# The first norms of a hybrid encoder block in a new order, with GpSimd's weight subtractions in eight pieces

## The chip, the cores and the metric

The kernel runs on one core of a Trainium2 chip. A core has a matrix engine (TensorE, in the profile PE for the products and PEld for its weight loads), VectorE (DVE), ScalarE (ACT), GpSimd (POOL) and SyncE (SP), whose queue issues most of the DMAs. Each engine works through its own list of instructions in a fixed order, and they wait for each other by semaphores. The metric is the device time of one execution in microseconds (us). The kernel before took 1527.0 us, the median of three runs (1525.58 to 1529.02).

## The reference

One block of depth 1 on 1040 tokens (16 learned meta tokens and 1024 frames) of width 1024, in float32. What matters here is the start of it:

```python
def rmsnorm(x, g):
    xf = x.astype(jnp.float32)
    y = xf * lax.rsqrt(jnp.mean(xf * xf, axis=-1, keepdims=True) + EPS)
    return (y * g.astype(jnp.float32)).astype(x.dtype)

def token_mixer(u, w_in, ...):
    proj = up @ w_in          # up: the normed stream, padded in front
    (ml_q, ml_k, ml_v, ml_o, ml_i, ml_f, rt_q, rt_k, rt_v, rt_g) = jnp.split(proj, offs, axis=-1)
    ...                       # mLSTM heads with gates, retention heads with rotary q and k
    return (mixed @ w_out)[:, n_pad:]

h = h + token_mixer(rmsnorm(h, norm_mix_g[l]), w_in[l], ...)
h = h + channel_mixer(rmsnorm(h, norm_ffn_g[l]), ...)
return rmsnorm(h, norm_final_g)[:, N_META:]
```

The stream is normed, projected to queries, keys, values, output gates and input/forget gates, run through four mLSTM heads and four retention heads, projected back, and followed by a gated MLP.

## The kernel before, in words

The stream lies transposed in SBUF: model width on the partitions (eight blocks of 128, in two tiles `x11` and `x12` for the first half of the tokens and `x21` and `x22` for the second), tokens along the free axis. To keep float32 accuracy in single-pass matmuls each operand is split in two parts, `hi` (a cast by ScalarE) and `lo` (the original minus `hi`, by VectorE or GpSimd), and a product is the sum of three: hi by hi, hi by lo, lo by hi.

The first norm goes through the tokens in five ranges r = 0 to 4 (`RNG`: 144, 128 and 256 tokens of the first half, 272 and 256 of the second). For each range:

- `norm_sums(r)`: the squares (`sqr`, by ScalarE, and for r < 2 by VectorE too), sums of squares by VectorE, a product with a column of ones on TensorE (`pca`, one column per 128 tokens), the root on ScalarE and the reciprocal on VectorE (`rcola`).
- `norm_split(r)`: the reciprocals are spread over the partitions by TensorE (`pra`, the rows), VectorE scales the stream (`scalar_tensor_tensor`, eight passes), ScalarE casts the high halves (`u11h`, `u12h`, ...), VectorE subtracts the low halves (`u11l`, ...).

What TensorE can do meanwhile are products of ranges that are ready: `v4_group(c)` makes the values and gate inputs of chunk c (`pv`, 48 matmuls of 264 columns; 8 chunks of 128 tokens, and the meta tokens as chunk 0), with weights `w0hi` and `w0lo` that `v0_split` makes; `q4_group(i, ...)` makes one head's queries (i = 0) or keys (i = 1) for a range of tokens (`pq`, 24 matmuls), with weights that `need(("q4", i))` loads and splits (`parts`: `hi_q` by ScalarE, `lo_q` by VectorE).

After the five ranges come sums and differences of the token blocks (`S1` to `S4`, for a Winograd-like scheme of the big products), their splits, the output gate of head 4 (`po4x`, `po4y`), the rotation of its queries and keys with two tables `A1` and `A2` (`tables_load`, 520 KB each, in buffers that the sums `s1` used before), and the gates: rows of input and forget gates through scans on VectorE (`gates`, `gsm`), a trip through a DRAM buffer `scr`, and then the chunkwise scan of the heads.

The order of instructions on each engine isn't that of the program text: the code is recorded and a scheduler of the framework (a timeline that it computes when the kernel is built) decides, by its own estimate of readiness, which recorded instruction of an engine comes next. `after(later, first)` adds an order between two instructions to what the data demand, and no wait of its own on the same engine. From the output gate of head 4 on (`dealt[0] = True`) the kernel's own planner deals out the work. `last[...]` keeps the latest instruction of a kind, for use in `after`.

The names in the lists of instructions carry a number for the range or the chunk: `pra4` are the rows of range 4, `pv4_5` the values of chunk 5, `pq40116` the queries of range (1, 16).

Of the kernel before, what the change touches and what calls it, by code (L numbers as in the profile page):

```python
# [10 lines left out]
F32 = mybir.dt.float32  # L11
# [6 lines left out]
P = 128  # L18
# [71 lines left out]
def body(ctx, tc, h_in, vecs, cst, mask_in, rot, w_v0, w_vp, w_g, w_out, w_up, w_gate, w_down, out):  # L90
# [381 lines left out]
    def parts(key, pairs, src):  # L472
        for i, (hi, lo) in enumerate(pairs):
            m = AC.copy(hi, src[:, i * HB:(i + 1) * HB])
            if not dealt[0]:
                after(m, last["first"])
        yield
        for i, (hi, lo) in enumerate(pairs):
            V.tensor_tensor(lo, src[:, i * HB:(i + 1) * HB], hi.bitcast(F32), ALU.subtract)
        done.add(key)  # L480

    def pairs_of(nm, n):
# [334 lines left out]
    def rms_sums(ss, t0, t1, nm, col, tag, more=()):  # L817
        n = t1 - t0
        o = n % P
        subs = ([(0, P, o)] if o else []) + [(i, P, P) for i in range(o, n, P)]  # L820
        pc = rps("pc" + nm, tag)
        for i, (o, w, _) in enumerate(subs):
            for a in (ss, *more):
                PE.matmul(pc[:w, i:i + 1], a[:, o:o + w], cs[:, C_M01 + P - 1:C_M01 + P], start=a is ss, stop=a is (ss, *more)[-1])
        ns = len(subs)
        last["sqrt"] = AC.activation(col[:, :ns], pc[:, :ns], AF.Sqrt, bias=epsc, scale=1.0 / D)
        last["recip"] = V.reciprocal(col[:, :ns], col[:, :ns])
        return n, subs, pc, col, nm

    def rms_rows(got, rb, tag):  # L830
        n, subs, pc, col, nm = got
        pr = rps("pr" + nm, tag)
        x = max(0, n - 512)
        for i, (o, _, w) in enumerate(subs):
            dst = pr[:, o - x:o - x + w] if o >= x else pc[:, 8:8 + w]
            PE.matmul(dst, col[:, i:i + 1].to_broadcast([P, P]), ident[:, :w], start=True, stop=True)
# [8 lines left out]

    norms = {}

    def norm_sums(r):
        half, j0, j1 = RNG[r]
        n = j1 - j0  # L850
        xs = [xf[f"{half + 1}{i + 1}"][:, :, j0:j1] for i in (0, 1)]
        sq = [x[:, :, j0:j1] for x in sqs]
        m = AC.activation(sq[0], xs[0], AF.Square)
        if r:
            after(m, last["sqrt"])
        if r < 2:
            m = V.tensor_tensor(sq[1], xs[1], xs[1], ALU.mult)
# [12 lines left out]
        norms[r] = xs, rms_sums(ss[0], 0, n, f"a{r}", tmp.tile([P, 5], F32, tag="rcol", name=f"rcola{r}"), "tr", ss[1:])  # L870

    def norm_split(r):
        half, j0, j1 = RNG[r]
        xs, got = norms.pop(r)
        pr = rms_rows(got, None, "upd")
        parts_ = [[u[:, :, j0:j1] for u in UB[f"{half + 1}{i + 1}"]] for i in range(2)]
        for i, x in enumerate(xs):
            for k in range(4):
                last["scale"] = V.scalar_tensor_tensor(x[:, k], x[:, k], vec[:, V_MIX + 4 * i + k:V_MIX + 4 * i + k + 1], pr, ALU.mult, ALU.mult)
            m = AC.copy(parts_[i][0], x)  # L880
# [24 lines left out]
    def v0_split():  # L905
        for i in range(2):
            after(AC.copy(w0hi[i], w0raw[i]), last["sqrt"])
            G.tensor_tensor(w0lo[i], w0raw[i], w0hi[i].bitcast(F32), ALU.subtract)

    def quads(dst, pv, n):  # L910
        yield
# [7 lines left out]
    def v4_group(c, tag, between=None):  # L919
        t0, L = CH[c]  # L920
        nv = 264
        pv = pp(f"pv4_{c}", tag)
        if c == 0:
            for i in range(2):
                for j in range(4):
                    PE.matmul(pv[32 * j:32 * j + 32, :nv], ug[:, 4 * i + j, :], w0raw[i][:, j * nv:(j + 1) * nv],
                                     start=i == 0, stop=i == 1, tile_position=(0, 32 * j))
            t = vz[:META, 264:264 + nv]
            spawn(quads(t, pv, nv))
            V.tensor_copy(gts[:META, :, 0, :], t[:, DV:].rearrange("p (a b) -> p a b", a=2))  # L930
            return
        half = c > 4
        j0 = t0 - 512 * half
        for i, j in ((0, 0), (0, 1), (1, 0)):
            if i and between:
                between()
            for kb in range(KB):
                u = UB[f"{half + 1}{kb // 4 + 1}"][i]
                o = kb % 4 * nv
                PE.matmul(pv[:, :nv], u[:, kb % 4, j0:j0 + L], (w0hi, w0lo)[j][kb // 4][:, o:o + nv], start=i + j + kb == 0, stop=i == 1 and kb == KB - 1, skip_group_check=True)  # L940
        AC.copy(vtile[4][half][:, (c - 1) % 4 * VW:(c - 1) % 4 * VW + DV], pv[:, :DV])
        V.tensor_copy(gts[:, :, c, :], pv[:, DV:nv].rearrange("p (a b) -> p a b", a=2))
# [818 lines left out]
    norm_sums(3)  # L1761
    for c in (3, 4):
        v4_group(c, next(ring0))
# [767 lines left out]
```

## Time and profile before

| | |
|---|---|
| median of 3 runs | 1527.0 us |
| the profiled execution: its own time, its span | 1527.2 us, 1525.4 us |
| TensorE busy | 1489.9 us, 98% of the span |
| VectorE busy | 1090.1 us, 71% |
| ScalarE busy | 755.6 us, 50% |
| GpSimd busy | 73.6 us, 5% |
| moved between HBM and SBUF | 161 GB/s over the span |

The profile is one execution. Times are counted from the start of the span. A row of the timeline gives start, length, engine, line, operation, written tile <- read tiles, shape, and how many like instructions were merged; in square brackets stands how long the engine had been idle and which instruction released it. A row of waits gives who waited for whom, the total, how often and the longest. A row of windows gives a stretch of time and the busy time of each engine in it, then the clock granted to TensorE, the DMA share and GB/s.

### The profile page before, as it was taken

The page shows a single profiled execution, that of the slowest core. Times are in us where ns is not written, and L with a number is a line of the kernel's source. Part 1 is how long each engine was busy: PE and PEld are TensorE (multiplying, and loading weights), DVE is VectorE, ACT ScalarE, POOL GpSimd, SP SyncE. Part 2 cuts the span into 40 slices and gives each one's busy share as a digit, 9 for nine tenths or more (in the row PEclk, how much of TensorE's full clock was granted, in tenths as well). Part 3 has the DMA queues.
Part 4 walks back from the last instruction along what each step waited for, and adds up shares of the span by engine and source line. Part 5 has one row for each costly group of instructions (what it writes and reads, how often), then busy time and mean ns, then how long its engine had stood idle before and what let it go on. Part 6 is the DMA issues. An engine that isn't in the chain of part 4 may idle for free.

```text
span 1525.4 us, 25488 instructions
## 1 busy us (share of the span) xinstructions
PE 1489.9 (98%) x9929; PEld 1350.0 (88%) x9929; DVE 1090.1 (71%) x2087; ACT 755.6 (50%) x1453; POOL 73.6 (5%) x153
## 2 busy tenths in 40 slices
PE   6999999999999999999999999999999999999997
PEld 6998999999999999986888988999999999888887
DVE  7785868678777677856867787767666666778657
ACT  4465655554655455553454565444444444444443
POOL 1000000000000000000000001222220000000000
PEclk9999999999999999999999999999999999999999
DMA  6022255323532355696333247888772224933313
GB/s 232 8 88 51 86 159 194 111 82 114 186 119 98 125 166 189 195 398 255 111 112 134 80 124 241 197 208 200 189 183 77 83 79 160 369 105 110 97 42 111
DMA packets 104586, 223.81 MB, mean 147 GB/s; under 512 B 10520, under 2 KB 33760, under 8 KB 104288
## 3 DMA queue, kind: packets, MB, share of 16 engines
q1 hardware_dynamic: 89824, 191.68, 37.7%
q0 software_dynamic: 8448, 23.07, 7.6%
q10 hardware_dynamic: 6192, 7.41, 1.4%
q8 instruction: 78, 1.28, 0.4%
q14 instruction: 44, 0.36, 0.1%
HBM read 178.05 MB, written 67.15 MB: 161 GB/s over the span
## 4 chain that ended last, share of the span: by engine, by line
PE 89%; DVE 6%; DMA 2%; ACT 2%; issue 1%; SPq 0%; DVEq 0%; ACTq 0%
PE pdx L902 3%; PE pdx L901 3%; PE pdx L900 3%; PE pup_x L901 2%; PE pup_x L902 2%; PE pga_x L900 2%; PE pup_x L900 2%; PE pga_x L901 2%; PE pga_x L902 2%; PE pdy L902 2%; PE pdy L901 2%; PE pdy L900 2%; PE n L1570 2%; PE pwx L902 2%; PE u L1568 2%; PE pv L940 2%
## 5 line engine op out<-in xcount | busy, mean ns | idle before, releaser
L780 ACT CAST hi_up<-raw_up 128x512 fp32r<-128x512 f32 (+1 forms) x52 | 36.4, 719 | 107.4 <-PE pga_z L901 61.1
L781 DVE TENSOR_TENSOR lo_ga<-fraw_ga,hi_ga 128x512 fp32r<-128x512 f32 (+1 forms) x52 | 41.9, 809 | 37.3 <-ACT hi_ga L780 37.1
L781 DVE TENSOR_TENSOR lo_up<-raw_up,hi_up 128x512 fp32r<-128x512 f32 (+1 forms) x52 | 41.3, 810 | 38.0 <-ACT hi_up L780 37.2
L900 PE MATMUL pup_x<-uh_g,hi_up 128*128 128x256 f32 (+1 forms) x240 | 67.2, 282 | 1.2 <-ACT uh_g L1928 1.2
L901 PE MATMUL pup_x<-ul_g,hi_up 128*128 128x256 f32 (+1 forms) x240 | 67.4, 282 | 0.1
L902 PE MATMUL pup_x<-uh_g,lo_up 128*128 128x256 f32 (+1 forms) x240 | 66.4, 282 | 0.0
L781 DVE TENSOR_TENSOR lo_d<-rd,hi_d 128x1024 fp32r<-128x1024 f32 (+1 forms) x34 | 37.7, 1114 | 32.8 <-ACT hi_d L780 32.7
L780 ACT CAST hi_ga<-fraw_ga 128x512 fp32r<-128x512 f32 (+1 forms) x52 | 36.4, 719 | 45.3 <-PE pup_z L901 21.9
L902 PE MATMUL pdx<-uh_d,lo_d 128*128 128x512 f32 (+1 forms) x156 | 57.9, 375 | 0.0
L901 PE MATMUL pdx<-ul_d,hi_d 128*128 128x512 f32 (+1 forms) x156 | 57.8, 374 | 0.0
L780 ACT CAST hi_d<-rd 128x1024 fp32r<-128x1024 f32 (+1 forms) x34 | 32.3, 959 | 49.3 <-PE pdy L901 32.5
L902 PE MATMUL pdy<-uh_d,lo_d 128*128 128x512 f32 x132 | 51.9, 393 | 0.0
L901 PE MATMUL pdy<-ul_d,hi_d 128*128 128x512 f32 x132 | 51.7, 392 | 0.0
L900 PE MATMUL pdx<-uh_d,hi_d 128*128 128x512 f32 (+1 forms) x156 | 48.5, 372 | 0.0
L900 PE MATMUL pdy<-uh_d,hi_d 128*128 128x512 f32 x132 | 47.9, 389 | 0.0
L900 PE MATMUL pga_x<-uh_g,hi_ga 128*128 128x512 f32 x120 | 47.5, 396 | 0.0
L901 PE MATMUL pga_x<-ul_g,hi_ga 128*128 128x512 f32 x120 | 47.5, 396 | 0.0
L900 PEld LDWEIGHTS pup_x<-uh_g,hi_up 128*128 128x128 f32 x240 | 45.3, 189 | 2.3 <-ACT uh_g L1928 1.4
L902 PE MATMUL pga_x<-uh_g,lo_ga 128*128 128x512 f32 x120 | 47.1, 393 | 0.0
L901 PEld LDWEIGHTS pup_x<-ul_g,hi_up 128*128 128x128 f32 x240 | 45.4, 189 | 1.0 <-DVE ul_g L1929 0.3
L902 PEld LDWEIGHTS pup_x<-uh_g,lo_up 128*128 128x128 f32 x240 | 44.8, 189 | 0.8
L1637 DVE SCALAR_TENSOR_TENSOR mx<-tr,vec,sig 128x386 f32<-128x386 f32 (+2 forms) x42 | 24.0, 572 | 20.7 <-PE tr L1629 16.0
(1684 smaller groups left out, 5752.4 us busy)
## 6 DMA issues: line engine op xcount, KB each, us to landing
raw_up<-w_up_d SPq DMA_DIRECT2D x22, 512.0 KB, 4.4
fraw_ga<-w_gate_d SPq DMA_DIRECT2D x22, 512.0 KB, 4.1
acts<-cv SPq DMA_DIRECT2D x44, 256.0 KB, 4.2
wsd<-w_down_d POOLq DMA_DIRECT2D x44, 256.0 KB, 6.6
rd<-wsd SPq DMA_DIRECT2D x22, 512.0 KB, 3.6
raw_w<-w_out_d SPq DMA_DIRECT2D x20, 512.0 KB, 6.8
wsw<-raw_w SPq DMA_DIRECT2D x32, 256.0 KB, 3.7
raw_m<-w_out_d SPq DMA_DIRECT2D x14, 512.0 KB, 4.0
```

Of the source, the lines that this page charges most:

```text
L780: AC.copy(hi[:, o:o + n], x)
L781: V.tensor_tensor(lo[:, o:o + n], x, hi[:, o:o + n].bitcast(F32), ALU.subtract)
L900: m.append(PE.matmul(pt, ah, xh_, start=first and k == 0, stop=False, skip_group_check=True))
L901: PE.matmul(pt, ah, xl_, start=False, stop=False, skip_group_check=True)
L902: m.append(PE.matmul(pt, al, xh_, start=False, stop=last and k == n - 1, skip_group_check=True))
L940: PE.matmul(pv[:, :nv], u[:, kb % 4, j0:j0 + L], (w0hi, w0lo)[j][kb // 4][:, o:o + nv], start=i + j + kb == 0, stop=i == 1 and kb == KB - ...
L1568: PE.matmul(up[:, :nv], kw[:L], v, start=True, stop=True)
L1570: PE.matmul(pn[:L, :nv], pt[:L, :L], v, start=True, stop=c == 0)
L1637: return V.scalar_tensor_tensor(dst, tr[:, x0 - t0:x1 - t0], vec[:, g:g + 1], sig(b, p)[:, x0 - a0:x1 - a0], ALU.mult, ALU.mult)
```

## The change

Six things are done in the first hundred microseconds, all in the code that records the first norms and products:

1. `v0_split`: GpSimd's two subtractions of 128 x 1056 become eight of 128 x 264.
2. The second range's sums and its rows (`norm_rows(1)`) are both placed inside the products of chunk 1, ahead of those with the low halves; those products are ordered behind the rows.
3. The query and key weights are asked for later (`need` moves behind the products of chunk 2), and their low halves (`lo_q`) are ordered behind the latest sum of squares.
4. The query and key products of the first 272 tokens are made together by `q4_pair`: pass by pass (hi by hi, hi by lo, lo by hi) for both, and not product by product for one and then the other.
5. The third range's sums stand between the second and the third pass, its rows between the queries and the keys of the third pass.
6. The later squares of ranges 2 and 3 are ordered behind the low halves before them (`last["pace"]`) instead of behind the reciprocal; the copy of the first keys stands behind the third range's cast.

The core of the diff:

```diff
@@ parts
-            V.tensor_tensor(lo, src[:, i * HB:(i + 1) * HB], hi.bitcast(F32), ALU.subtract)
+            m = V.tensor_tensor(lo, src[:, i * HB:(i + 1) * HB], hi.bitcast(F32), ALU.subtract)
+            if not dealt[0]:
+                after(m, last["added"])
@@ norm_sums
-                after(m, last["recip"])
-            V.tensor_tensor(sq[0][:, 0:2], sq[0][:, 0:2], sq[0][:, 2:4], ALU.add)
+                after(m, last["pace"] if r in (2, 3) else last["recip"])
+            last["added"] = V.tensor_tensor(sq[0][:, 0:2], sq[0][:, 0:2], sq[0][:, 2:4], ALU.add)
...
+    def norm_rows(r):
+        norms[r] += (rms_rows(norms[r][1], None, "upd"),)
@@ v0_split
-            G.tensor_tensor(w0lo[i], w0raw[i], w0hi[i].bitcast(F32), ALU.subtract)
+            for o in range(0, 1056, 264):
+                G.tensor_tensor(w0lo[i][:, o:o + 264], w0raw[i][:, o:o + 264], w0hi[i][:, o:o + 264].bitcast(F32), ALU.subtract)
@@ v4_group
+                if i and between:
+                    after(m, last["rows"])
@@ new
+    def q4_pair(half, j0, j1, tags, between):
+        w = [need(("q4", i), 1 - i) for i in range(2)]
+        pt = [pp(f"pq4{i}{half}{j0}", tags[i])[:, :j1 - j0] for i in range(2)]
+        for p, (a, b) in enumerate(((0, 0), (0, 1), (1, 0))):
+            if p == 2:
+                between()
+            for i in range(2):
+                if p == 2 and i:
+                    norm_rows(2)
+                for kb in range(KB):
+                    u = UB[f"{half + 1}{kb // 4 + 1}"][b]
+                    m = PE.matmul(pt[i], w[i][kb // 4][a][:, kb % 4 * P:(kb % 4 + 1) * P], u[:, kb % 4, j0:j1], start=p + kb == 0, stop=p == 2 and kb == KB - 1, skip_group_check=True)
+                    if p == 2:
+                        after(m, last["rows" if i else "sums"])
+        AC.copy(raws[0][:, half * 512 + j0:half * 512 + j1], pt[0])
+        yield
+        after(AC.copy(raws[1][:, half * 512 + j0:half * 512 + j1], pt[1]), last["cast"])
@@ the first products
-    v4_group(1, next(ring0), lambda: norm_sums(1))
-    need(("q4", 0), 1)
+    def second():
+        norm_sums(1)
+        norm_rows(1)
+    v4_group(1, next(ring0), second)
     norm_split(1)
     v4_group(0, next(ring0))
     v4_group(2, next(ring0))
-    norm_sums(2)
-    q4_group(0, 0, 0, 272, next(ring0))
+    third = norm_sums(2, True)
+    need(("q4", 0), 1)
+    pair = q4_pair(0, 0, 272, [next(ring0), next(ring0)], third)
+    next(pair)
     norm_split(2)
-    q4_group(1, 0, 0, 272, next(ring0))
+    next(pair, None)
```

What becomes of it on the engines is decided by the scheduler. Behind the first hundred microseconds the lists of the two kernels are the same but for two products in the middle of TensorE's. At three places they differ in what the prediction speaks of.

VectorE's list from the second range's squares on, before: `sqr1` the squares, `u11l` and `u12l` the low halves of the first range, `lo_q4` the weights' low halves, `rcola1` and `rcola2` the reciprocals of ranges 1 and 2.

```order
L857 TENSOR_TENSOR sqr1_133<-x12_121 128x4x128
L887 COPY ug_117<-x11_122 128x128
L884 TENSOR_TENSOR u11l_125<-x11_122,u11h_124 128x4x144
L887 COPY ug_117<-x12_121 128x128
L884 TENSOR_TENSOR u12l_127<-x12_121,u12h_126 128x4x144
L479 TENSOR_TENSOR lo_q4_0_0_290<-raw_q4_0_201,hi_q4_0_0_289 128x512 x2
L479 TENSOR_TENSOR lo_q4_1_0_298<-raw_q4_1_203,hi_q4_1_0_297 128x512 x2
L827 RECIPROCAL rcola1_267<-rcola1_267 128x1
L865 TENSOR_TENSOR sqr0_132<-sqr0_132,sqr1_133 128x4x256
L868 TENSOR_TENSOR sqr0_132<-sqr0_132 128x2x256
```

The same place of VectorE's list now:

```order
L895 TENSOR_TENSOR u12l_127<-x12_121,u12h_126 128x4x144
L829 RECIPROCAL rcola1_273<-rcola1_273 128x1
L890 SCALAR_TENSOR_TENSOR x11_122<-x11_122,vec_72,pra1_285 128x128 x4
L890 SCALAR_TENSOR_TENSOR x12_121<-x12_121,vec_72,pra1_285 128x128 x4
L956 COPY gts_116<-pv4_1_254 128x2x4
L927 TENSOR_TENSOR vz_111<-pv4_0_309,vz_111 16x264
L895 TENSOR_TENSOR u11l_125<-x11_122,u11h_124 128x4x128
L927 TENSOR_TENSOR vz_111<-pv4_0_309,vz_111 16x264
L895 TENSOR_TENSOR u12l_127<-x12_121,u12h_126 128x4x128
L867 TENSOR_TENSOR sqr0_132<-sqr0_132,sqr1_133 128x4x256
L927 TENSOR_TENSOR vz_111<-pv4_0_309,vz_111 16x264
L870 TENSOR_TENSOR sqr0_132<-sqr0_132 128x2x256
```

The reciprocals and the scaling of range 1 moved ahead of the weights' low halves, which now follow behind these rows.

TensorE's list at the rows of the last range (`pra4`), before:

```order
L891 MATMUL pq410272_562<-u12l_127,hi_q4_1_0_297 128x256
L892 MATMUL pq410272_562<-u12h_126,lo_q4_1_0_298 128x256
L836 MATMUL pra4_588<-cs_73,rcola4_528 128x128 x2
L940 MATMUL pv4_5_631<-w0hiq_106,u21h_130 128x264 x4
L940 MATMUL pv4_5_631<-w0hik_107,u22h_128 128x264 x4
L940 MATMUL pv4_5_631<-w0lo0_108,u21h_130 128x264 x4
L940 MATMUL pv4_5_631<-w0lo1_109,u22h_128 128x264 x4
```

and now, where the values of chunks 5 and 6 and the first queries of the second half come first (46 and 12 matmuls in all):

```order
L901 MATMUL pq40116_691<-u21h_130,hi_q4_0_0_354 128x256
L902 MATMUL pq40116_691<-u21l_131,hi_q4_0_0_354 128x256
L952 MATMUL pv4_5_637<-w0hik_107,u22l_129 128x264 x4
L952 MATMUL pv4_6_664<-w0hik_107,u22l_129 128x264 x2
L838 MATMUL pra4_594<-cs_73,rcola4_534 128x128 x2
L952 MATMUL pv4_6_664<-w0hik_107,u22l_129 128x264 x2
```

The last range's rows moved behind nearly all products of chunks 5 and 6.

SP's list of DMAs behind the loads of the stream, before (`A1_4` and `A2_4` are the rotation tables, `raw_q0a`, `raw_vp0` and `raw_q0b` weights):

```order
L328 DMA raw_o4b_303<-w_g_d 128x512 x2
L1102 DMA A1_4_851<-rot_d 128x1040
L1103 DMA A2_4_852<-rot_d 128x1040
L328 DMA raw_q0a_873<-w_g_d 128x1024
L328 DMA raw_vp0_21_1262<-w_vp_d 128x1024
L328 DMA raw_vp0_22_1264<-w_vp_d 128x1024
```

and now:

```order
L328 DMA raw_o4b_368<-w_g_d 128x512 x2
L328 DMA raw_q0a_879<-w_g_d 128x1024
L328 DMA raw_vp0_21_1268<-w_vp_d 128x1024
L328 DMA raw_vp0_22_1270<-w_vp_d 128x1024
L1134 DMA A1_4_857<-rot_d 128x1040
L1135 DMA A2_4_858<-rot_d 128x1040
```

The tables moved behind three weight loads, two of which wait for products of TensorE.

More of the change, by code (lines that the diff above doesn't have):

```diff
@@ L823, in rms_sums @@
             for a in (ss, *more):
-                PE.matmul(pc[:w, i:i + 1], a[:, o:o + w], cs[:, C_M01 + P - 1:C_M01 + P], start=a is ss, stop=a is (ss, *more)[-1])
+                last["sums"] = PE.matmul(pc[:w, i:i + 1], a[:, o:o + w], cs[:, C_M01 + P - 1:C_M01 + P], start=a is ss, stop=a is (ss, *more)[-1])
         ns = len(subs)
@@ L835, in rms_rows @@
             dst = pr[:, o - x:o - x + w] if o >= x else pc[:, 8:8 + w]
-            PE.matmul(dst, col[:, i:i + 1].to_broadcast([P, P]), ident[:, :w], start=True, stop=True)
+            last["rows"] = PE.matmul(dst, col[:, i:i + 1].to_broadcast([P, P]), ident[:, :w], start=True, stop=True)
         if x:
@@ L846, in body, with norm_sums @@
     norms = {}
-    def norm_sums(r):
+    def norm_sums(r, late=False):
         half, j0, j1 = RNG[r]
@@ L866, in norm_sums, with sums @@
             if r:
-                after(m, last["recip"])
-            V.tensor_tensor(sq[0][:, 0:2], sq[0][:, 0:2], sq[0][:, 2:4], ALU.add)
+                after(m, last["pace"] if r in (2, 3) else last["recip"])
+            last["added"] = V.tensor_tensor(sq[0][:, 0:2], sq[0][:, 0:2], sq[0][:, 2:4], ALU.add)
             ss = [sq[0][:, k] for k in range(2)]
-        norms[r] = xs, rms_sums(ss[0], 0, n, f"a{r}", tmp.tile([P, 5], F32, tag="rcol", name=f"rcola{r}"), "tr", ss[1:])
+        def sums():
+            norms[r] = xs, rms_sums(ss[0], 0, n, f"a{r}", tmp.tile([P, 5], F32, tag="rcol", name=f"rcola{r}"), "tr", ss[1:])
+        if late:
+            return sums
+        sums()
+    def norm_rows(r):
+        norms[r] += (rms_rows(norms[r][1], None, "upd"),)
     def norm_split(r):
         half, j0, j1 = RNG[r]
-        xs, got = norms.pop(r)
-        pr = rms_rows(got, None, "upd")
+        if len(norms[r]) < 3:
+            norm_rows(r)
+        xs, got, pr = norms.pop(r)
         parts_ = [[u[:, :, j0:j1] for u in UB[f"{half + 1}{i + 1}"]] for i in range(2)]
@@ L879, in norm_split @@
                 last["scale"] = V.scalar_tensor_tensor(x[:, k], x[:, k], vec[:, V_MIX + 4 * i + k:V_MIX + 4 * i + k + 1], pr, ALU.mult, ALU.mult)
-            m = AC.copy(parts_[i][0], x)
+            m = last["cast"] = AC.copy(parts_[i][0], x)
             if r == 0:
@@ L939, in v4_group @@
                 o = kb % 4 * nv
-                PE.matmul(pv[:, :nv], u[:, kb % 4, j0:j0 + L], (w0hi, w0lo)[j][kb // 4][:, o:o + nv], start=i + j + kb == 0, stop=i == 1 and kb == KB - 1, skip_group_check=True)
+                m = PE.matmul(pv[:, :nv], u[:, kb % 4, j0:j0 + L], (w0hi, w0lo)[j][kb // 4][:, o:o + nv], start=i + j + kb == 0, stop=i == 1 and kb == KB - 1, skip_group_check=True)
+                if i and between:
+                    after(m, last["rows"])
         AC.copy(vtile[4][half][:, (c - 1) % 4 * VW:(c - 1) % 4 * VW + DV], pv[:, :DV])
```

## The prediction

> **What bounds the kernel now.** I read the page first, then the table by windows, then the timeline of the first 125 us, since the list of instructions changes only there.
>
> ```profile
> span 1525.4 us, 25488 instructions
> PE 1489.9 (98%) x9929; PEld 1350.0 (88%) x9929; DVE 1090.1 (71%) x2087; ACT 755.6 (50%) x1453; POOL 73.6 (5%) x153
> PE   6999999999999999999999999999999999999997
> ```
>
> TensorE is busy in 98% of the span, and one of its weakest slices is the first. A change in the first 100 us counts only by how much later or earlier it lets TensorE go on for the rest. The windows of that stage (PE, PEld, DVE, ACT, POOL busy; then granted clock, DMA share, GB/s):
>
> ```profile
> 28.00:31.50 3.50, 3.50 (x17) 3.50 (x18) 3.47 (x9) 2.44 (x4) 0.09 (x1) 0.51 0.03 7
> 35.00:40.00 5.00, 5.00 (x44) 5.00 (x43) 4.20 (x6) 1.15 (x3) 0.00 (x0) 1.00 0.00 0
> 53.40:84.50 31.10, 30.52 (x261) 29.58 (x261) 29.39 (x39) 17.22 (x27) 3.30 (x2) 1.00 0.16 52
> ```
>
> From 28 to 31.5 TensorE works at half its clock. From 53.4 to 84.5 it is full, but VectorE too: 29.39 of 31.10 us. That second queue is what the change runs into.
>
> **The front, 0 to 53 us.** The waits that the new order is about:
>
> ```profile
> 12.49 2.44 POOL L908 TENSOR_TENSOR w0lo<-w0raw,w0hik 128x1056 fp32r<-128x1056 f32 x1
> 12.79 2.68 DVE L857 TENSOR_TENSOR sqr<-x 128x512 f32<-128x512 f32 x1
> 15.54 1.87 PE L824 MATMUL pca<-cs,sqr 128*128 128x1 f32 x8 [0.99 <-DVE sqr L857]
> 17.01 2.49 DVE L479 TENSOR_TENSOR lo_q<-raw_q,hi_q 128x512 fp32r<-128x512 f32 x4
> 26.24 0.71 PE L836 MATMUL pra<-cs,rcola 128*128 128x128 f32 x4 [1.22 <-DVE rcola L827]
> 27.88 1.08 PE L940 MATMUL pv<-w0hiq,u11h 128*128 128x264 f32 x4 [0.93 <-ACT u11h L880]
> ```
>
> VectorE's square of the second range took 2.68 us, where a product of that shape takes 2.49 / 4 = 0.62: it ended 15.47, 0.5 us after GpSimd's subtraction (14.93). In pieces of 2.44 / 4 = 0.61 us it need wait for one piece only: 12.79 + 0.61 + 0.62 = 14.0. That removes TensorE's wait of 0.99. Bounds: 0.99, or nothing if VectorE stays out until all eight pieces are through. I take 0.99.
> The Trainium skill's page "SBUF — State Buffer" (section "Who interferes with whom") says that a VectorE instruction with two SBUF inputs and a GpSimd instruction that reads SBUF exclude each other for a whole instruction, whichever issued first. This trace agrees with the 2.68; no row yet shows which of the two goes next between two pieces.
>
> The third range's squares, sums and rows now come behind the first query and key products, so the waits 1.22 and 0.93 go, and with them, if nothing else stops TensorE, the half clock: 3.5 x 0.49 = 1.7 us. New waits come, from these rows:
>
> ```profile
> 23.50 2.15 DVE L879 SCALAR_TENSOR_TENSOR x<-x,vec,pra 128x128 f32<-128x128 f32 x8 [0.41 <-PE pra L836]
> 27.22 0.61 ACT L880 CAST u11h<-x 128x512 fp32r<-128x512 f32 x1
> 28.68 1.66 DVE L879 SCALAR_TENSOR_TENSOR x<-x,vec,pra 128x256 f32<-128x256 f32 x4
> 30.37 1.05 ACT L880 CAST u11h<-x 128x1024 fp32r<-128x1024 f32 x1 [0.98 <-DVE x L879]
> 52.78 0.61 PE L836 MATMUL pra<-cs,rcola 128*128 128x128 f32 x4
> 53.42 3.22 DVE L879 SCALAR_TENSOR_TENSOR x<-x,vec,pra 128x256 f32<-128x256 f32 x8 [0.99 <-PE pra L836]
> 53.71 0.65 PE L940 MATMUL pv<-w0hik,u22h 128*128 128x264 f32 x4
> 58.57 0.65 PE L940 MATMUL pv<-w0hik,u22l 128*128 128x264 f32 x4
> ```
>
> From a row multiply to its first scaling pass 53.42 - 52.78 = 0.64 us. A matmul takes (58.57 - 53.71) / 40 = 0.12. After the second range's rows TensorE has 8 products and a ninth small one (1.3 us) before it needs the new high half: 0.64 + 2.15 / 2 + 0.61 = 2.3, so 1.0 of waiting. After the third's it has the two row multiplies and 8 query-low products (0.5 + 1.0): 0.64 + 1.66 + 1.05 = 3.35, so 1.9. Each can be 0.5 longer, where ScalarE still has casts and copies queued ahead. The front: -0.99 - 1.22 - 0.93 - 1.7 + 1.0 + 1.9 = -1.9 us (from -3.0, were the new waits half as long, to about 0, were the clock to fall again). GpSimd's eight starts for two, and 24 + 24 products in another order, cost TensorE nothing else: the number of matmuls is the same.
>
> **The last norm, 53 to 88 us.** Before, the rows of the last range (52.78) stand ahead of the value products of chunks 5 and 6. Now 58 matmuls stand ahead of them: 46 value and 12 query and key products, 58 x 0.12 = 7.0 us. They come at 52.78 + 7.0 - 1.9 = 57.9, and VectorE scales from 58.5 on instead of 53.4: 5.1 later. It has idled before that, but what follows is the same list of work: two differences, low halves, sums, four more low halves, up to the rotation. VectorE's waits in that stretch:
>
> ```profile
> DVE gates L1213 <- ACT gates L1212: 2.2, 1, 2.2
> DVE x L879 <- PE pra L836: 1.0, 1, 1.0
> DVE uS1l L1787 <- ACT uS1h L1786: 0.8, 1, 0.8
> DVE uS3l L1787 <- ACT uS3h L1786: 0.5, 1, 0.5
> DVE gts L942 <- ACT v4hi L941: 0.3, 1, 0.3
> ...
> ```
>
> A later VectorE no longer waits for the last three: -1.6. No other idle time can take up the lag; 3.5 of 5.1 us remain. (Bounds: 5.1 if nothing is swallowed; nothing at all if the scaling starts 3.5 earlier than I find.)
>
> **The rotation tables.** SP's queue has them behind three weight loads now:
>
> ```profile
> 73.96 0.33 SPq L1102 DMA_DIRECT2D A<-rot_d  x1
> 75.12 0.33 SPq L1103 DMA_DIRECT2D A<-rot_d  x1
> 83.55 0.80 SPq L328 DMA_DIRECT2D raw_vp<-w_vp_d  x2
> 84.46 0.70 DVE L1180 TENSOR_TENSOR qT<-rawq,A 128x528 f32<-128x528 f32 x1
> ...
> A<-rot_d SPq DMA_DIRECT2D x2, 520.0 KB, 4.7
> raw_vp<-w_vp_d SPq DMA_DIRECT2D x2, 512.0 KB, 4.5
> raw_q0a<-w_g_d SPq DMA_DIRECT2D x1, 512.0 KB, 3.6
> ```
>
> Before, they landed some 5 us ahead of their use (75.12 + 4.7 against 84.46). Now they follow raw_vp, which waits for TensorE's meta products: 83.55 - 1.9 and, as TensorE meets VectorE's lag, perhaps a microsecond more. Issued at some 83.5 and landed 4.7 to 5.7 later, behind 1.5 MB of the other loads, they come at 88.2 to 89.2; VectorE is ready at 84.46 + 3.5 = 88.0. I take 1.0 us of waiting (0 if they land first, 1.7 if both come last).
>
> **To the end.** Why TensorE follows VectorE here:
>
> ```profile
> 88.45 1.28 ACT L1212 ACT_TABLE_LOAD   x1
> 89.75 0.36 ACT L1212 ACTIVATE gates<-pg,gsm 36x128 f32<-36x128 f32 x1
> 106.91 0.38 SPq L1267 DMA_DIRECT2D scr<-gates  x1
> 124.08 0.80 PE L1523 MATMUL s<-qT,kT 128*128 128x128 f32 x2 [2.62 <-DVE pt L1547]
> PE pe L1240 <- DVE gsm L1236: 0.8, 1, 0.8
> PE pe L1239 <- DVE gates L1232: 0.6, 1, 0.6
> PE s L1523 <- DVE pt L1547: 2.6, 1, 2.6
> ```
>
> Rotation, gate rows, scans, the trip of the gates through memory (106.91) and the first scan step are one chain on VectorE. TensorE waits for it three times (0.6, 0.8, 2.6), so a gain of TensorE ahead of it only lengthens these waits, and a lag of the chain arrives whole. ScalarE's table load and tanh (1.28 + 0.36) make the gate wait 1.8 instead of 2.2: -0.4. Sum: 5.1 - 1.6 + 1.0 - 0.4 = +4.1 us. The profiled execution took 1527.2 us (1.8 around the span); 1527.2 + 4.1 = 1531.3, and as it lies 0.2 over the median of 1527.0, I predict 1531.1.
>
> **Rivals.** (1) The other side: the front decides. If the last scaling starts by 55.0 (53.42 + 1.6), VectorE swallows the lag, and the front's gain stays: 1527.0 - 1.9 = 1525.1. VectorE's 71% speaks for it, the 29.39 of 31.10 against it. Chance 0.12. (2) The tables land in time: 1530.1; the 3.6 us of a single load speaks for it. Chance 0.13. (3) The clock halves again after the new wait of 1.9, as in 28 to 31.5 after waits of 1.22 and 0.93: 1.7 more, and the last norm as much later, 1532.8. Chance 0.20. The Trainium skill's page "TensorE: Matmul & The Clock Gate" (section "Part 1: The HAM clock gate") says that activity is judged in free-running windows of 3.4 us, so where the wait falls changes from one execution to the next; the 3.5 us at 0.51 agree with its length. (4) The pieces do not let VectorE in: the 0.99 stays, 1532.1. Chance 0.10. The forecast itself, from 1529.5 to 1532.8, has 0.45.
>
> **How the numbers follow.** A measurement can tell about 0.2% (3.05 us) from no change. Above 1530.05 lie three quarters of the forecast, half of (2), all of (3) and (4): 0.70. Rival (1) is within 0.2% unless the clock also stays up throughout: 0.06 faster, 0.24 the same. The range takes in rival (1) at its own value and rival (3) with longer waits of 0.5 each and the tables' 0.7: 1525.0 to 1534.5.
>
> **What would show it.** Right: VectorE's square of the second range at 0.6 to 1.3 us; TensorE full and at full clock from about 21 to 34, then a wait of about 1.9 for the third high half; the last scaling at about 58.5; qT at 88 to 90, with a DMA as releaser; waits of TensorE between 75 and 100 us some 5 us longer in all than the 0.6 of before. Wrong: a scaling that starts by 55, or a rotation that starts by 85.

## The result and the profile after

The changed kernel took 1535.7 us (median of 6 runs, 1533.2 to 1537.9), the kernel before on the same chip 1527.6 (6 runs, 1525.6 to 1529.1): a ratio of 1.0054, 95% interval 1.0040 to 1.0068, or 8.2 us more. The prediction said slower, by 4.1 us, with a range up to 1534.5: the sign was right, the size half of what came. The profiled execution of the changed kernel took 1534.5 us, with a span of 1532.7, 7.3 us longer than that of before.

From its page:

```profile
span 1532.7 us, 25492 instructions
PE 1491.9 (97%) x9929; PEld 1351.0 (88%) x9929; DVE 1089.5 (71%) x2087; ACT 754.8 (49%) x1453; POOL 84.7 (6%) x159
```

TensorE and VectorE do the same work. GpSimd does not: 84.7 us where it had 73.6. The same three windows as before, the last one moved with the last scaling and ended where VectorE runs dry (columns as in the prediction: PE, PEld, DVE, ACT, POOL, then clock, DMA share, GB/s):

```profile
28.00:31.50 3.50, 3.50 (x30) 3.50 (x30) 3.48 (x7) 0.38 (x1) 0.00 (x0) 1.00 0.03 4
35.00:40.00 5.00, 2.96 (x23) 2.66 (x22) 5.00 (x11) 3.88 (x7) 0.00 (x0) 1.00 0.04 15
60.00:90.60 30.60, 27.01 (x228) 25.67 (x227) 28.78 (x37) 17.39 (x28) 12.39 (x2) 1.00 0.20 65
```

The half clock at 28 to 31.5 is gone (30 products where there were 17), and 2 us of it are given back at 35 to 40. In the third window TensorE, which was full there (30.52 of 31.10), idles 3.6 us, in waits for ScalarE (1.0 and 1.2) and VectorE (1.4).

The front, from the timeline: the square that GpSimd had held up, GpSimd's second four pieces, and TensorE's two new waits.

```profile
13.05 0.72 DVE L859 TENSOR_TENSOR sqr<-x 128x512 f32<-128x512 f32 x1
13.19 3.83 POOL L920 TENSOR_TENSOR w0lo<-w0raw,w0hik 128x264 fp32r<-128x264 f32 x4
24.99 0.76 PE L952 MATMUL pv<-w0hiq,u11h 128*128 128x264 f32 x4 [0.98 <-ACT u11h L891]
37.60 1.24 PE L952 MATMUL pv<-w0hiq,u11h 128*128 128x264 f32 x8 [2.04 <-ACT u11h L891]
```

Square 0.72 us, waits 0.98 and 2.04: as forecast (0.6 to 1.3, 1.0, 1.9). From the last norm on, in order of time:

```profile
40.60 1.28 DVE L867 TENSOR_TENSOR sqr<-sqr,sqr 128x1088 f32<-128x1088 f32 x1
56.55 0.15 DVE L829 RECIPROCAL rcola<-rcola 128x2 f32<-128x2 f32 x1
59.36 0.61 PE L838 MATMUL pra<-cs,rcola 128*128 128x128 f32 x4
60.00 3.22 DVE L890 SCALAR_TENSOR_TENSOR x<-x,vec,pra 128x256 f32<-128x256 f32 x8
74.04 12.39 POOL L1844 COPY s<-x 128x1056 f32<-128x1056 f32 x2 [42.34 <-DVE gts L956]
82.06 2.42 DVE L1823 TENSOR_TENSOR uS1l<-s,uS1h 128x1056 fp32r<-128x1056 f32 x2
84.43 0.38 SPq L1134 DMA_DIRECT2D A<-rot_d  x1
84.90 0.38 SPq L1135 DMA_DIRECT2D A<-rot_d  x1
86.63 1.26 DVE L1823 TENSOR_TENSOR uS4l<-s,uS4h 128x1056 fp32r<-128x1056 f32 x1 [1.81 <-ACT uS4h L1822]
93.72 0.71 DVE L1212 TENSOR_TENSOR qT<-rawq,A 128x528 f32<-128x528 f32 x1 [3.12 <-DMA A<-rot_d]
99.70 0.34 DVE L1245 TENSOR_SCALAR gates<-pg,vec 36x128 f32<-36x128 f32 x1 [1.77 <-ACT gates L1244]
116.47 0.38 SPq L1299 DMA_DIRECT2D scr<-gates  x1
```

Against before: the last rows 59.36 for 52.78 (+6.6), the rotation 93.72 for 84.46 (+9.3), the gates 99.70 for 90.14 and their trip through memory 116.47 for 106.91 (both +9.6). TensorE then gets some 2 us back, for the most part since its clock does not halve behind the first scan step as it did before:

```profile
125.00:130.00 5.00, 5.00 (x27) 4.42 (x27) 3.32 (x9) 1.11 (x3) 0.00 (x0) 0.79 0.02 3
```

is the window of before there (120 to 125 us had 0.87); in the changed kernel all windows from 120 to 145 us have 1.00. This need not be the change's doing. TensorE's wait at that step is 2.2 to 2.7 us in eleven of the fourteen traces of this case; the clock halved behind it in six of them, the kernel before among them, and not in the five others, the changed kernel among them.

### The profile page after: what moved, and what is told of

It is laid out like the page before. It is cut to its first block, busy times and chain, and to the rows that moved or that the text cites. A ratio compares the mean times of both kernels' runs of the same rounds, so it can differ in the third digit from the quotient of the medians.

```text
span 1532.7 us, 25492 instructions
## 1 busy us (share of the span) xinstructions
PE 1491.9 (97%) x9929; PEld 1351.0 (88%) x9929; DVE 1089.5 (71%) x2087; ACT 754.8 (49%) x1453; POOL 84.7 (6%) x159
## 4 chain that ended last, share of the span: by engine, by line
PE 88%; DVE 6%; DMA 3%; ACT 2%; issue 1%; SPq 0%; DVEq 0%; ACTq 0%
PE pdx L913 3%; PE pdx L912 3%; PE pdx L911 3%; PE pup_x L912 2%; PE pup_x L913 2%; PE pup_x L911 2%; PE pga_x L911 2%; PE pga_x L912 2%; PE pga_x L913 2%; PE pdy L913 2%; PE pdy L912 2%; PE pdy L911 2%; PE n L1602 2%; PE pwx L913 2%; PE u L1600 2%; PE pwx L911 2%
## 5 line engine op out<-in xcount | busy, mean ns | idle before, releaser
L662 POOL DMA_DIRECT2D wsd<-w_down_d x33 | 19.9, 748 | 383.4 <-DVE s2up L2192 382.7
```

The lines of the kernel that those rows point to most:

```text
L662: dep(G.dma_start(x, y), last["pace"], True)
```

## The experiments

Two theories stood against each other at first. T: the rotation tables' late landing sets the end. L: the order of the added squares behind the low halves (part 6 of the change, one argument of one `after`) makes the late ranges late, and the rest follows. Two things were open besides: what GpSimd's pieces are worth, and what its long copies cost. All ratios are to the kernel before, run on the same chip beside them, with 95% intervals; in the three sets of runs its median was 1527.8, 1527.2 and 1528.1 us. Kernels of different sets are compared by their ratios (0.001 is 1.5 us); these are estimates over all runs of a set and differ from the quotients of the medians by up to 0.001.

### The tables first

```diff
@@ tables_load
-            nc.sync.dma_start(A2, rot[:, 1])
+            last["tables"] = nc.sync.dma_start(A2, rot[:, 1])
@@ jput
-            nc.sync.dma_start(x[:, o:o + y.shape[1]], y)
+            m = nc.sync.dma_start(x[:, o:o + y.shape[1]], y)
+            if nm in ("q0a", "vp0_21", "vp0_22") and "tables" in last:
+                after(m, last["tables"])
```

> The changed kernel with one edit: SP's list has the two rotation tables ahead of the three weight loads again, as before the change. Theory T (the tables set the end): in the changed kernel VectorE is done with its list at 90.60 and stands 3.12 us for the first table. If the tables are issued as soon as VectorE has read their buffers (about 83.3 and 84.5 us) and land 5 to 6 us later, the rotation starts at about 90.6, limited by VectorE, and the time falls by about 3 us, to some 1532.5. Theory L (the late last norm sets the end, and the tables only come last in that lag): the same 3 us at most, and at least 5 us of the loss stay. Rival: the weight loads, now later, become what TensorE waits for (they feed the casts from 96 us on), and the time stays at 1535 to 1536.

1533.2 us, ratio 1.0038 (1.0024 to 1.0051): 2.4 us of the loss. SP's queue and VectorE:

```profile
83.76 0.33 SPq L1134 DMA_DIRECT2D A<-rot_d  x1
90.79 0.70 DVE L1212 TENSOR_TENSOR qT<-rawq,A 128x528 f32<-128x528 f32 x1
```

The rotation no longer waits. The tables cost about what VectorE stood for them (3.12), and the larger part of the loss stays, as L says and T doesn't.

### The order behind the low halves: undone, and alone

Undone in the changed kernel:

```diff
@@ norm_sums
-                after(m, last["pace"] if r in (2, 3) else last["recip"])
+                after(m, last["recip"])
```

> The changed kernel with one part undone: the added squares of ranges 2 and 3 are ordered behind the reciprocal again, as before the change, and not behind the low halves of the range before. Theory L: this order is what makes the third range's rows late (33.94 us instead of 26.24), and all later ranges with them. Undone, the third rows come at 27 to 29 us, the last rows at 50 to 52.5, the tables are issued at about 73, and the time is 1524 to 1528, 8 to 11 us under the changed kernel. Theory T: the last norm matters little, and a gain of at most 3 us comes from the tables. Rival P (the gain or loss is the GpSimd pieces' and the pass-by-pass products'): within 2 us of the changed kernel.

1529.6 us, ratio 1.0014 (1.0005 to 1.0023): 6.1 us of the loss are gone. Less than L had it, and the third rows came at 33.27 us in this trace and not at 27 to 29. Their reciprocal was there at 27.89, so the order no longer held them; TensorE did, which waited longer for the second range's high half,

```profile
30.41 1.25 PE L952 MATMUL pv<-w0hiq,u11h 128*128 128x264 f32 x4 [2.85 <-ACT u11h L891]
```

and then worked at half its clock (0.50 in the window from 29 to 32 us). The rest of what is left is taken up below. The scheduler puts the tables ahead of the weights again by itself, and GpSimd's copies take 3.43 us.

Alone, the same line put into the kernel before (there it replaces `last["recip"]`):

> The kernel before with one part of the change alone: the added squares of ranges 2 and 3 are ordered behind the low halves of the range before. Theory L (this order makes the late ranges late, whatever else is changed): the third rows move from 26.2 to 33 us or later, the last rows from 52.8 to 58 us or later, the tables are issued behind 83 us, and the time rises by 6 to 10 us, to 1534 to 1538. Rival C (the order does harm only together with the pass-by-pass products): less than 3 us, under 1531.

1534.6 us, ratio 1.0048 (1.0035 to 1.0061). One line in the kernel before brings nearly the whole loss. In its trace:

```profile
36.47 0.61 PE L836 MATMUL pra<-cs,rcola 128*128 128x128 f32 x4
42.60 1.29 DVE L865 TENSOR_TENSOR sqr<-sqr,sqr 128x1088 f32<-128x1088 f32 x1
61.98 1.26 DVE L879 SCALAR_TENSOR_TENSOR x<-x,vec,pra 128x256 f32<-128x256 f32 x3 [3.24 <-PE pra L836]
87.54 0.37 SPq L1102 DMA_DIRECT2D A<-rot_d  x1
```

Rows of the third range, added squares of the fourth, last scaling, tables: all as late as in the changed kernel or later, without pieces or products pass by pass. The tables stand behind the weight loads here too, and GpSimd's copies take 12.38 us. So L holds, and rival C of that expectation falls: it is this order, whatever else is changed.

### The last rows ahead of the values

```diff
@@ v4_group
-                if i and between:
+                if i and between or c in (5, 6):
                     after(m, last["rows"])
```

> The changed kernel with one edit: the value products of chunks 5 and 6 are ordered behind the rows of the last range. The scheduler then also puts the tables ahead of the weights. Theory L: the last scaling starts 1 to 3 us earlier than 60.0, and the time is 1530 to 1532.5, a gain that is mostly the tables' (2.5 us in the run with the tables first) and to a lesser part the earlier rows'. My prediction's step (58 products ahead of the last rows make the lag of 7.0 us): with those out of the way the scaling starts at 54 to 55 and the time comes down to 1527 to 1529. Rival: TensorE waits for the rows instead, and the time stays at 1535.

1530.9 us, ratio 1.0029 (1.0020 to 1.0037). In the trace:

```profile
59.16 0.16 DVE L829 RECIPROCAL rcola<-rcola 128x2 f32<-128x2 f32 x1
60.76 0.61 PE L838 MATMUL pra<-cs,rcola 128*128 128x128 f32 x4
61.41 3.22 DVE L890 SCALAR_TENSOR_TENSOR x<-x,vec,pra 128x256 f32<-128x256 f32 x8 [1.43 <-PE pra L838]
85.42 0.33 SPq L1134 DMA_DIRECT2D A<-rot_d  x1
```

With the 58 products out of the way the last scaling does not start at 54 or 55. Now VectorE waits 1.43 for the rows, which stand behind query and key products, and before the reciprocal at 59.16 they could not have come. (In this execution all is later from the start; from the rows of the third range, 36.55, to the last scaling it takes 24.9 us, in the changed kernel 60.00 - 33.94 = 26.1.) From the start of the last reciprocal to the rows it takes 2.89 us in the kernel before (52.78 - 49.89), 2.81 in the changed kernel (59.36 - 56.55) and 1.60 here. So the 58 products lengthened nothing there against before: the whole lag of 6.6 us stands in the reciprocal already (56.55 for 49.89), and 1.2 us is what came back when they were out of the way. The gain of 3.8 us (by the ratios) came with the tables, ahead of the weights here too, and with GpSimd's copies, which took 5.7 us; how it divides between these two and the 1.2 us of earlier scaling wasn't measured.

### GpSimd's long copies

```diff
@@ the fourth sum (in the kernel with the tables first)
-        G.tensor_copy(x12[i], part("12", i))
+        AC.copy(x12[i], part("12", i))
```

> The kernel of the run with the tables first, with one edit more: the two copies of 128x1056 that GpSimd makes for the fourth sum (12.39 us there, 3.30 in the kernel before) are made by ScalarE. Theory G (VectorE's back-to-back instructions keep GpSimd out, and the fourth sum's halves come late by it): VectorE's wait of 1.8 us for uS4h goes, the rotation starts at 88.5 to 89.2 instead of 90.8, and the time falls by 1 to 2 us from 1533.2. Rival: ScalarE, which gets 2.1 us of copies at a stage where it is full, hands on the same delay, and the time stays within 0.7 us.

1531.4 us, ratio 1.0028 (1.0017 to 1.0039), 1.5 us under the kernel with the tables first. The intervals overlap, so the times alone don't show the gain. The traces show that a wait went. With the copies on GpSimd (tables first), then on ScalarE:

```profile
86.91 1.26 DVE L1823 TENSOR_TENSOR uS4l<-s,uS4h 128x1056 fp32r<-128x1056 f32 x1 [1.81 <-ACT uS4h L1822]
```

```profile
84.37 2.43 DVE L1823 TENSOR_TENSOR uS1l<-s,uS1h 128x1056 fp32r<-128x1056 f32 x2
86.71 1.26 DVE L1823 TENSOR_TENSOR uS4l<-s,uS4h 128x1056 fp32r<-128x1056 f32 x1
90.91 0.72 DVE L1212 TENSOR_TENSOR qT<-rawq,A 128x528 f32<-128x528 f32 x1
```

VectorE's wait of 1.81 is gone. From the last scaling to the rotation it takes 90.91 - 62.32 = 28.6 us instead of 90.79 - 60.29 = 30.5. (The rotation was expected at 88.5 to 89.2; this execution was some 2 us late before the last scaling already, for its clock came up late, as the last section tells.)

### GpSimd's pieces

Four kernels. The change without the pieces, and the kernel before with them alone:

```diff
@@ v0_split (in the changed kernel)
-            for o in range(0, 1056, 264):
+            for o in range(0, 1056, 1056):
@@ v0_split (in the kernel before)
-            G.tensor_tensor(w0lo[i], w0raw[i], w0hi[i].bitcast(F32), ALU.subtract)
+            for o in range(0, 1056, 264):
+                G.tensor_tensor(w0lo[i][:, o:o + 264], w0raw[i][:, o:o + 264], w0hi[i][:, o:o + 264].bitcast(F32), ALU.subtract)
```

> The changed kernel with one part undone: GpSimd's weight subtractions in two instructions of 128x1056. Rival P (the pieces hold VectorE up: copies of 0.77 for 0.21 us and low halves of 1.32 for 0.75 us between 13.7 and 17.6): faster by 0.5 to 1.5 us. My prediction's step: VectorE's square takes 2.68 us again, TensorE waits 0.99 us longer, and the time rises by 0.5 to 1.5 us if the lag is handed on, by nothing if the half clock of the first 21 us swallows it.

> The kernel before with one part of the change alone: GpSimd's weight subtractions in eight pieces of 128x264. By my prediction's step VectorE's square of the second range falls from 2.68 to 0.7 us, TensorE's wait of 0.99 us at 15.5 goes, and the time falls by up to 1 us, 1526.5 to 1527.5. Rival: VectorE's copies and low halves behind the square now meet a piece each (0.56 us four times), and nothing is gained: 1527 to 1529.

The change without pieces: 1536.0 us, 1.0064 (1.0048 to 1.0081), not to be told from the change. The pieces alone: 1530.7 us, 1.0012 (0.9999 to 1.0024): no gain, and rather a loss, though VectorE's square takes 0.72 us and TensorE's wait of 0.99 is gone. What goes on instead stands in TensorE's timeline. The meta tokens' products (128*32) and the second low half, with the pieces alone:

```profile
18.85 1.09 PE L926 MATMUL pv<-w0raw,ug 128*32 128x264 f32 x2
19.87 0.59 PE L940 MATMUL pv<-w0lo,u12h 128*128 128x264 f32 x1
20.39 1.09 PE L926 MATMUL pv<-w0raw,ug 128*32 128x264 f32 x4
```

and in the kernel before:

```profile
19.30 1.11 PE L926 MATMUL pv<-w0raw,ug 128*32 128x264 f32 x8
20.34 1.16 PE L940 MATMUL pv<-w0lo,u12h 128*128 128x264 f32 x4
```

Since the low halves come piece by piece, the scheduler deals their four products out singly among the meta tokens' products. Eight records of these in a row take 1.11 us; two of them between others take 1.09, and so do four. The changed kernel has the same mix at 18 to 22 us. Putting the meta tokens' products behind the low half again:

```diff
@@ v4_group
-                    PE.matmul(pv[32 * j:32 * j + 32, :nv], ug[:, 4 * i + j, :], ...)
+                    after(PE.matmul(pv[32 * j:32 * j + 32, :nv], ug[:, 4 * i + j, :], ...), last["hl"])
...
+                if c == 1 and j: last["hl"] = m
```

in the kernel before with the pieces,

> The kernel before with GpSimd's eight pieces, as in the run with the pieces alone (1530.7 against 1527.8), and one edit more: TensorE's products of the meta tokens (128*32) are ordered behind the four products of the second low half, which the pieces had led the scheduler to deal out singly among them. Theory M (the mix costs: four of the meta products take 1.02 us between single products where eight in a row took 1.04, and the clock comes up later): the stretch from 17.6 to the rows of the second range is 2 us shorter, and the time is 1525.5 to 1527.5. Rival (the pieces themselves cost, by VectorE's waits for them): it stays at 1529 to 1531.

and in the changed kernel:

> The changed kernel with only the mix undone (meta products behind the four products of the second low half). Theory M with theory L: TensorE reaches the second range's rows 1 to 2 us earlier, but they are not late in the list that sets the end; the chain from the third range's rows to the tables moves by what TensorE gains, and the time falls by 0.5 to 2 us, 1533.5 to 1535.5. If the mix were the main loss: 1530 or less.

In the kernel before 1527.4 us, 0.9995 (0.9987 to 1.0003): the loss is gone, no gain is left. In the changed kernel 1534.5 us, 1.0049 (1.0035 to 1.0063), 0.8 us less than the change, well within the intervals. So the pieces bring nothing measurable when unmixed. A gain of 1 us is not excluded: in the trace of the kernel before with unmixed pieces the last scaling starts at 52.47 and the rotation at 83.50, 0.95 and 0.96 us earlier than before, as the prediction's step has it.

Mixed, their price depends on the kernel: 1.8 us in the kernel before (the interval reaches from -0.2 to 3.7), 3.7 us in the change without its order (1.0014 above, 0.9990 below), and nothing that can be told in the change, perhaps because the order holds everything up there anyway. Part of it may be the clock and not the mix: in the trace of the pieces alone the clock came up only at about 25 us, and of its eleven executions three took 1525.7 to 1526.3 us and eight 1529.3 to 1531.8. The 38 records from the second sums to the last of the meta tokens' products take 9.8 us there, 6.9 unmixed and 6.8 in the kernel before (clock up at about 21 in both), and 7.9 in the changed kernel, mixed with the clock up at about 19.3. So by these single traces some 1 us is the mix's own; the rest wasn't separated from the clock.

The Trainium skill's page "TensorE: Matmul & The Clock Gate" (section "Part 3: Packing small matmuls — row/col tiling") says that products on different groups of 32 columns run at the same time when they follow each other. The rows agree: the meta tokens' products go to four such groups, and those that stand alone between full ones take as long as four side by side.

### Without the order, and what is left to gain

The changed kernel with the order undone, in three forms: without pieces; with pieces, but unmixed; the latter with the long copies on ScalarE.

> The changed kernel with two parts undone, the order behind the low halves and GpSimd's pieces. If the pieces are the rest of the loss (1529.6 against 1527.8 with the order alone undone; the pieces alone cost the kernel before about 1.9), the time is 1526.5 to 1528.5. If the products pass by pass and the later query lows are the rest, it stays at 1529 to 1530.5.

> The changed kernel without the order behind the low halves, as in the run with that part undone (1529.6), and with the meta products ordered behind the four products of the second low half. The pieces stay. Theory M: the time falls to that of the kernel without pieces (1524.7), less up to 1 us for the wait of 0.99 that the pieces remove: 1523.5 to 1525.5. Rival: the pieces themselves cost, and it stays at 1528.5 to 1530.

> The changed kernel without the order behind the low halves, with the meta products behind the four products of the second low half, and with the two copies of 128x1056 on ScalarE instead of GpSimd. Where the tables are early and VectorE leaves gaps, GpSimd's copies took 3.4 us and nobody waited for them, so by theory G this changes nothing against the same kernel with the copies on GpSimd: within 0.7 us of it, 1523 to 1526. Rival: it frees VectorE by another 0.5 us and more, as it did with the tables first (1.9 us).

1524.7 us, 0.9990 (0.9981 to 1.0000); 1527.0, 0.9996 (0.9987 to 1.0005); 1525.9, 0.9992 (0.9983 to 1.0002). All three are level with the kernel before or up to 0.2% below it. The first, the change without its order and without its pieces, has the lowest ratio of all kernels run; whether it beats the kernel before is on the edge of what these runs can tell. The pieces did not bring the 1 us that was expected over it, and the copies on ScalarE changed nothing where VectorE leaves gaps, as theory G said. In the first the list runs about as it did before (last scaling at 53.42, tables at 73.96, rotation at 84.46), 0.7 to 0.8 us later, so its lower time does not come from this stage:

```profile
30.71 1.06 PE L838 MATMUL pra<-cs,rcola 128*128 128x128 f32 x4
54.24 3.23 DVE L890 SCALAR_TENSOR_TENSOR x<-x,vec,pra 128x256 f32<-128x256 f32 x8 [0.71 <-PE pra L838]
74.79 0.33 SPq L1134 DMA_DIRECT2D A<-rot_d  x1
85.15 0.70 DVE L1212 TENSOR_TENSOR qT<-rawq,A 128x528 f32<-128x528 f32 x1
```

With these runs, four pairs of kernels differ in the order alone. By the ratios it costs 7.3 us in the kernel before, 6.1 in the change, 8.1 in the change unmixed (1.0049 and 0.9996) and 11.3 in the change without pieces (1.0064, of five runs, and 0.9990). In the unmixed pair the last scaling, with the order and then without it:

```profile
59.22 3.22 DVE L890 SCALAR_TENSOR_TENSOR x<-x,vec,pra 128x256 f32<-128x256 f32 x8
```

```profile
52.26 3.22 DVE L890 SCALAR_TENSOR_TENSOR x<-x,vec,pra 128x256 f32<-128x256 f32 x8 [0.70 <-PE pra L838]
```

Of these 7.0 us, 0.7 are there at the second range's rows already (20.89 and 20.20), ahead of the order.

## Why the prediction was right in sign and half in size

It named the chain rightly: last scaling, VectorE's list, tables, rotation, gates, and TensorE behind it. The steps that failed are three of its terms. The start of the last scaling was put down to the 58 products, and the order of part 6 was left out (+6.6 for +5.1); the swallowed waits left out GpSimd's copies (-0.4 for -1.6); the tables were given 4.7 to 5.7 us to land and took 9.3 and 10.1 (+3.1 and +0.6 for +1.0). With the gate wait the measured terms give 6.6 - 0.4 + 3.1 + 0.6 - 0.4 = 9.5 us, of the 9.6 by which the gates came late; 2.3 of these came back at the end, which makes the 7.3 us of the span. Term by term, against the trace after:

- **Front, -1.9.** The waits of 0.99, 1.22 and 0.93 and the half clock went, the new ones were 0.98 and 2.04, all as forecast. Yet the last rows came at 59.36, and 52.78 + 7.0 - 59.36 leaves a gain of only 0.4. The step that failed here is "cost TensorE nothing else: the number of matmuls is the same". The stretch from the second sums to the last of the meta tokens' products, the same 38 records, before and then after:

```profile
17.27 1.23 PE L940 MATMUL pv<-w0hik,u12h 128*128 128x264 f32 x4
...
23.40 0.65 PE L926 MATMUL pv<-w0raw,ug 128*32 128x264 f32 x6
```

```profile
16.16 1.23 PE L952 MATMUL pv<-w0hik,u12h 128*128 128x264 f32 x4
...
23.38 0.63 PE L938 MATMUL pv<-w0raw,ug 128*32 128x264 f32 x2
```

  TensorE enters it 1.1 us earlier and leaves it at the same time (24.05 and 24.01): the mix takes the whole gain of the square. The clock is not the reason, since it came up earlier in this execution than in that of before (at about 19.3 and 21). The order of the list showed the mix; I counted products there, not groups.
- **Start of the last scaling, +5.1.** Measured +6.6 (60.00 for 53.42). The cause that was given, 58 products ahead of the rows, is not the cause, and that the size came out near is luck: from the last reciprocal to the rows it takes 2.8 us, as before (2.9). TensorE filled with these products the time in which the reciprocal was late, and with them out of the way the scaling came only 1.2 us sooner. The cause is the order that part 6 adds, whose queue I did not follow. The added squares wait for low halves, these for a cast, a scaling and the rows of the range before, and so each range hands its lateness to the next. The third range's rows come at 33.94 for 26.24, the fourth range's squares are added at 40.60 for 27.35, and the last reciprocal comes at 56.55 for 49.89. Before:

```profile
27.35 1.29 DVE L865 TENSOR_TENSOR sqr<-sqr,sqr 128x1088 f32<-128x1088 f32 x1 [0.24 <-ACT sqr L861]
49.89 0.16 DVE L827 RECIPROCAL rcola<-rcola 128x2 f32<-128x2 f32 x1
```

  The order alone costs the kernel before 7.3 us, where the whole change costs 8.2. Which of the two ranges' orders weighs more was not run.
- **Swallowed waits, -1.6.** VectorE was done with its list at 89.31 + 1.29 = 90.60, 6.1 later than before: of the lag of 6.6 only 0.4 was swallowed. The three waits did go, but a new one of 1.81 came, for a fourth sum that GpSimd's copies delivered late. No row of before shows it: the copies took 3.30 there,

```profile
69.39 3.30 POOL L1808 COPY s<-x 128x1056 f32<-128x1056 f32 x2 [38.84 <-PE pv L940]
```

  beside a VectorE that paused (0.34 and 0.81 us in that stretch). The timeline could have shown that they would now fall into a stretch without a pause.
- **Tables, +1.0.** Measured 3.12, and 0.64 for the second. The landing was put at 88.2 to 89.2; it was at 93.7. They were issued at 84.43 and 84.90, not 83.5: SP was issuing the two loads ahead of them until 84.34 (83.53 + 0.81), and the trace shows no other wait of SP there. Without these loads the first could have gone some 1 us sooner, the second hardly, since VectorE reads their buffers (`uS1l`) until 83.3 and 84.4; this bound stood in no term. And they took 9.3 and 10.1 us to land instead of the 4.7 to 5.7 allowed, behind three loads of 512 KB. With the tables first, 2.4 us came back.
- **Gate wait, -0.4.** Right: 1.77 for 2.20.
- **The end.** The chain's lag of 9.6 became 7.3 in the span. That 1.7 of it would come back (5 x 0.13 + 5 x 0.21, from the two windows of before), through a clock that does not halve at 125 us, stood in no term; as other traces have it either way, it may belong to the execution.

Of the rivals, (1), the front decides, falls: the last scaling starts at 60.00, not by 55. (2), tables in time, falls. (3), a second half clock behind the wait of 2.04, did not come in this execution, nor in four others with the same wait; it did come in the trace of the change without pieces (0.53 from 41 to 44 us), whose 1539.5 us are the highest of its five times. (Later, at 90 to 95 and 100 to 105 us, the clock did halve in the changed kernel, windows at 0.66; TensorE was idle for part of the windows behind these, busy 2.80 and 4.11 of 5.00 us, so it had time to spare there.) (4) falls as it was worded, since the pieces did let VectorE in; its price, a front without the 0.99, was nearly paid all the same, on another engine. The range ended at 1534.5, 1.2 us too low: the later start, the slower copies and the later tables came together, and of these only the tables had a bound of their own in it (0.7 more).

## What to carry to other kernels

An order between two instructions that adds no wait where it is written can still hold up all that stands behind it on that engine; follow the delayed result through every engine to the next place where something is late, before looking at what was moved. Here one such line cost 6 to 8 us in three pairs of kernels, and 11 in a fourth. When a producer is cut into pieces, look at what the scheduler does with its consumers: the pieces were as fast as forecast, and their products, dealt out one by one, took the gain back.

## What the runs showed of the hardware

- **GpSimd kept out by a full VectorE.** The first of the two copies of 128x1056 took 11.38 us, the second 1.06 (shortest and longest of that line in the changed kernel's trace; in the kernel before 2.29 and 1.06). The first began at 74.04 and ended at 85.42, 1.0 us behind the end of the last of eleven back-to-back instructions of VectorE with two SBUF tiles as inputs (84.40); the instruction that followed reads `po4y`, a product's accumulator. In some ten changes from one VectorE instruction to the next GpSimd was not let in. In the front it went the other way: between 13 and 18 us VectorE's low halves of the first range took 1.32 instead of 0.75 us, where GpSimd's pieces run beside them (13.19 to 17.02).

```profile
14.39 1.32 DVE L895 TENSOR_TENSOR u11l<-x,u11h 128x576 fp32r<-128x576 f32 x1
16.31 1.32 DVE L895 TENSOR_TENSOR u12l<-x,u12h 128x576 fp32r<-128x576 f32 x1
```

  The Trainium skill's page "SBUF — State Buffer" (section "Who interferes with whom") says that the two exclude each other and that the order of issue decides. Both places agree with the first; which of the two comes next after an instruction differed between them, and no run here shows what decides it.
- **The clock at the start.** In the fourteen executions with a trace, products of 264 columns went from 0.22 to 0.12 us each at some time between 19 and 25.3 us, read from these durations, while the column of the granted clock says 1.00 throughout. Of the six with the mix (the changed kernel's is one), four came up only at about 25; the eight without it were all up by 23.3. Whether the mix is the cause stays open with so few. It moves what follows by up to 2.5 us from one execution to another.
